# Down projections of three feed-forward layers: three of four quarters by seven block products instead of eight

## The chip, the cores and the metric

The kernel runs on one core of a Trainium2 chip. The metric is the device time of one execution in microseconds (us), smaller is better. All data are float32; the outputs are 512 tokens x 1024 features.

The core's engines are named as in the profile: PE (TensorE, matrix products into PSUM), PEld (its weight loads, which overlap PE), DVE (VectorE), ACT (ScalarE), POOL (GpSimd) and SP (SyncE, which here issues the loads from HBM). Each engine works through a queue of its own in order; where an instruction waits for another engine, everything behind it on its queue waits too.

## What is computed

Two blocks are applied to 512 tokens: the first once, the second twice (`DEPTH_2 = 2`). Each has a mixing part (attention and a linear recurrence) and then a feed-forward layer. Only the feed-forward layers are touched by the change; there are three of them, of the same shape:

```python
D_MODEL = 1024
SEQ = 512
D_FF = 4 * D_MODEL
...
        n2 = rms_norm(h, norm2_g[layer])
        h = h + jnp.square(jax.nn.relu(n2 @ w_up[layer])) @ w_down[layer]
...
    hid = jnp.square(jax.nn.relu(jnp.einsum('bsd,df->bsf', x, w_ff1)))
    ff = jnp.einsum('bsf,fd->bsd', hid, w_ff2)
    return layernorm(DEEPNORM_ALPHA * x + ff, ln2_g, ln2_b)
```

So a layer is an up projection (512 x 1024 by 1024 x 4096), a squared relu, and a down projection (512 x 4096 by 4096 x 1024), added to the residual.

## The kernel before, in words

**Matrix products.** A float32 operand x is split in two parts of a narrower kind, hi (a copy by ACT, `copy`) and lo = x - hi (a subtraction by DVE, `sub_lo`); `split2` does both. A product is then three matmuls, hi by hi, hi by lo and lo by hi, accumulated in one PSUM bank. Every matmul here takes 128 rows of contraction and writes 128 x 512.

**Weights.** `wblk` loads one block of 128 x 1024 by a DMA on SP into a tile `wr` (3 buffers), copies it into `wh` (ACT) and subtracts into `wl` (DVE). `wh` and `wl` have 6 buffers each (`NW = 6`), so weights can be split up to six blocks ahead of the block that PE works on.

**Up projection.** A block of `form_a` makes 128 of the 4096 hidden features for all 512 tokens: 8 steps of contraction x 3 matmuls = 24 matmuls from one weight block. `finish` then does relu (ACT), the square (POOL) and the split of the result into `uh` (ACT) and `ul` (DVE).

**Down projection.** `ffn` works in two halves of the hidden features: 16 up blocks, then `proj_b` twice (output columns 0 to 511 and 512 to 1023). `proj_b` holds four PSUM banks, one for each 128 tokens; each weight block covers 256 hidden features by 512 columns and feeds 2 x 3 matmuls per bank. After the last step `add_to` adds each bank to the residual tile `h` on DVE (8 additions per half).

**Who sets the order.** The order on PE is written out by hand: generators are resumed by a small planner (class `Weave`) that books costs and due times; PE then keeps that order. The order on ACT, DVE, POOL and SP is made by the scheduler of the framework, which also hands out buffers and places the semaphores. Most small tiles, activations among them, come from one pool of 56 buffers of 128 x 512 (`bt`). PSUM has 8 banks: four for projections (`mm_ps`) and four for attention and transposes (`at_ps`).

All helpers record their instructions at two places: L310 is every matmul, L262 every instruction of ACT, DVE and POOL. So rows are told apart by their tiles.

Of the kernel before, what the change touches and what calls it, by code (L numbers as in the profile page):

```python
# [11 lines left out]
F32R = mybir.dt.float32r  # L12
I32 = mybir.dt.int32
AF = mybir.ActivationFunctionType
ALU = mybir.AluOpType
# [4 lines left out]
P, T, D = 128, 512, 1024  # L20
# [133 lines left out]
class Event:  # L154


    t = None
# [110 lines left out]
def model_kernel(ctx: ExitStack, tc: tile.TileContext, I, out):  # L268
    nc = tc.nc
# [3 lines left out]
    pw = ctx.enter_context(tc.tile_pool(name="pw", bufs=NW))  # L273
# [8 lines left out]
    wv = Weave(8 - NM)  # L282
    act, dve, pool = Engine(nc.scalar, wv, 0.2, 0.83), Engine(nc.vector, wv, 0.17, 1.04), Engine(nc.gpsimd, wv, 0.25, 2.1)
    uid = [0]

    def nm(s):
        uid[0] += 1
        return f"{s}_{uid[0]}"

    def bt(s="b", dt=F32):  # L290
        return pb.tile([P, T], dt, tag="b", name=nm(s))

    def at(s="a", dt=F32):
        return pa.tile([P, 4, T], dt, tag="a", name=nm(s))
# [6 lines left out]
    def mm_ps():  # L301
        return psm.tile([P, T], F32, tag="mm", name=nm("mm"))

    def at_ps():
        t = psa.tile([P, T], F32, tag="at", name=nm("at"))
        wv.bank(t)
        return t

    def mm(out, lhsT, rhs, start, stop):
        nc.tensor.matmul(out, lhsT, rhs, start=start, stop=stop)  # L310
        n = rhs.free_size()
        if lhsT.dtype == F32:
            c = max(4 * n, 1024 if n < P else 0) * (0.5 if lhsT.free_size() <= 64 else 1.0)
        else:
            c = n if n >= 256 else 4 * n
        wv.now += c / 2400.0
# [96 lines left out]
    def proj_a(name, l, c, acts, k=8):  # L413
        ps = mm_ps()
        yield from form_a(ps, wblk(name, l, 0, k * P, c, c + P), 0, acts, range(k))
        return ps

    def proj_b(name, l, k0, k1, c, acts, done, koff=0, tail=0, wait_k=False, wait_t=False, pre=None):


        pss = [mm_ps() for _ in range(NT)]
        ks = list(range(k0 // P, k1 // P))
        steps = [ks[i : i + 2] for i in range(0, len(ks) - tail, 2)] + ([ks[len(ks) - tail :]] if tail else [])
        for st in steps:
            if pre is not None:
                pre(st[0])
            pieces = 2 if pre is not None and st[0] == 0 else 1
            ws = [wblk(name, l, k * P, (k + 2) * P, c, c + 512, pieces=pieces) for k in st[::2]]
            if pre is not None:
                pre(st[1])  # L430
            if wait_k:
                for k in st:
                    yield acts.ev[k - koff]
            for t in range(NT):
                if wait_t:
                    yield acts.ev[t]
# [174 lines left out]
    def add_to(res, n, alpha, part=None, then=None):  # L611


        def done(t, ps):
            wv.fork()
            h = res[t][n]
            if alpha == 1.0:
                dve.tensor_tensor(h, ps, h, ALU.add)
            else:
                dve.scalar_tensor_tensor(h, h, alpha, ps, ALU.mult, ALU.add)  # L620
            if part is not None:
                part(t, n)
            if then is not None:
                wv.spawn(then(t), 0)

        return done

    def out_proj(name, l, acts, res, alpha, part, then):
        yield from proj_b(name, l, 0, D, 0, acts, add_to(res, 0, alpha, part), wait_k=True)
        yield from proj_b(name, l, 0, D, 512, acts, add_to(res, 1, alpha, part, then), tail=8)  # L630

    def ffn(up, down, l, acts, res, alpha, part, then):
        for half in range(2):
            u = Acts(16, "u")

            def finish(f, ps):
                wv.fork()
                a, b = bt("ua"), bt("ub")
                act.activation(a, ps, AF.Relu)
                pool.tensor_tensor(b, a, a, ALU.mult)  # L640
                u.split(f, b)

            f0 = 0
            if half == 0:
                f0 = 4
                ws = [wblk(up, l, 0, D, P * f, P * f + P) for f in range(f0)]
                pss = [mm_ps() for _ in range(f0)]
                for j in range(2):
                    for t in range(2):
                        yield acts.ev[2 * j + t]  # L650
                    for f in range(f0):
                        yield from form_a(pss[f], ws[f], 0, acts, range(8), slice(256 * j, 256 * j + 256))
                for f in range(f0):
                    finish(f, pss[f])
            for f in range(f0, 16):
                ps = yield from proj_a(up, l, 2048 * half + P * f, acts)
                finish(f, ps)
            for n in range(2):
                last = half and n
                yield from proj_b(  # L660
                    down, l, 2048 * half, 2048 * half + 2048, 512 * n, u,
                    add_to(res, n, 1.0 if half else alpha, part if half else None, then if last else None),
                    koff=16 * half, tail=8 if last else 0, wait_k=True,
                )

    def norm_rows(g, b, l):
        return [[row_bcast(I[x], D * l + 512 * n) for n in range(2)] for x in (g, b)]
# [570 lines left out]
```

## Time and profile before

| | |
|---|---|
| median of 3 runs | 2087.22 us (2085.84 to 2088.24) |
| the profiled execution's own time | 2085.96 us |
| its span, first to last instruction | 2083.9 us |
| PE busy | 2037.8 us, 98% of the span |
| DVE busy | 939.8 us, 45% |
| ACT busy | 808.5 us, 39% |
| POOL busy | 342.7 us, 16% |
| DMA queue, share of 16 engines | 29.3% |

The three feed-forward layers are the longest stretches of the profile in which PE is never idle; between them lie the attention parts. The profile names, for every group of instructions, the busy time, the mean time of one and the idle time before it. The timeline lists single instructions with start and duration; neighbours of an engine can overlap a little, since the next one starts while the last one drains.

### The profile page before, as it was taken

The numbers are of one execution on the slowest core, as the hardware profiler recorded it, in microseconds if no ns is written. First come the engines' busy times: TensorE is split into PE (matmuls) and PEld (weight loads), VectorE is DVE, ScalarE is ACT, GpSimd is POOL, SyncE is SP. The second block draws the span as 40 slices with busy tenths as digits, with TensorE's granted clock in tenths as the row PEclk, the third lists the DMA queues.
The fourth block names the chain that finished last, engine by engine and source line by source line (L and its number), as shares of the span: only waits on it lengthen the run. The fifth ranks groups of instructions, "written<-read, shape, count | busy, mean of one in ns | idle before, by whom it ended". The sixth has DMA issues, their size and how long they took to land.

```text
span 2083.9 us, 24530 instructions
## 1 busy us (share of the span) xinstructions
PE 2037.8 (98%) x9694; PEld 1685.6 (81%) x9694; DVE 939.8 (45%) x1602; ACT 808.5 (39%) x1261; POOL 342.7 (16%) x313
## 2 busy tenths in 40 slices
PE   8999899999999999999999999999999999999998
PEld 7777778889888888877888888888877878888886
DVE  6676444544323332475555322324675554323333
ACT  6565344433422331364334322322564333322321
POOL 2000000001300210020413200311111422201302
PEclk9999999999999999999999999999999999999999
DMA  5431112242323322332232323222422233323231
GB/s 196 152 112 61 44 69 95 97 151 78 106 94 98 101 92 91 112 107 75 77 112 91 101 92 101 96 96 71 137 92 81 72 111 102 101 91 101 94 98 41
DMA packets 62371, 202.67 MB, mean 97 GB/s; under 512 B 7279, under 2 KB 7745, under 8 KB 62257
## 3 DMA queue, kind: packets, MB, share of 16 engines
q1 hardware_dynamic: 62256, 201.12, 29.3%
q8 instruction: 76, 1.25, 0.2%
q14 instruction: 39, 0.31, 0.0%
HBM read 198.94 MB, written 4.77 MB: 98 GB/s over the span
## 4 chain that ended last, share of the span: by engine, by line
PE 92%; DVE 2%; ACT 2%; POOL 2%; issue 1%; DMA 0%; POOLq 0%; ACTq 0%; DVEq 0%; SPq 0%
PE mm L310 84%; PE at L310 5%; PE at L319 2%; POOL h L262 1%; POOL mv L262 1%; ACT wh L262 0%; DVE wl L262 0%; DVE h L262 0%; ACT h L262 0%; ACT kh L262 0%; DVE og L262 0%; ACT qs L262 0%; DVE qs L262 0%; ACT sil L262 0%; DVE bs L262 0%
## 5 line engine op out<-in xcount | busy, mean ns | idle before, releaser
L262 DVE TENSOR_TENSOR wl<-wr,wh 128x1024 fp32r<-128x1024 f32 (+1 forms) x337 | 424.1, 1259 | 646.1 <-ACT wh L262 644.8
L262 ACT ACTIVATE wh<-wr 128x1024 fp32r<-128x1024 f32 (+1 forms) x340 | 358.8, 1057 | 769.9 <-PE mm L310 742.4
L310 PE MATMUL mm<-hTh,wh 128*128 128x512 f32 (+1 forms) x864 | 317.5, 367 | 0.0
L310 PE MATMUL mm<-hTl,wh 128*128 128x512 f32 (+1 forms) x864 | 316.7, 367 | 0.0
L310 PE MATMUL mm<-hTh,wl 128*128 128x512 f32 (+1 forms) x864 | 316.6, 366 | 0.0
L310 PE MATMUL mm<-wh,uh 128*128 128x512 f32 x768 | 299.1, 390 | 0.0
L310 PE MATMUL mm<-wl,uh 128*128 128x512 f32 x768 | 298.8, 389 | 0.0
L310 PE MATMUL mm<-wh,ul 128*128 128x512 f32 x768 | 298.8, 389 | 0.0
L262 POOL TENSOR_TENSOR ub<-ua 128x512 f32<-128x512 f32 x96 | 153.2, 1596 | 642.2 <-ACT ua L262 642.2
L310 PE MATMUL mm<-xTh,wh 128*128 128x512 f32 x536 | 214.1, 399 | 0.0
L310 PE MATMUL mm<-xTl,wh 128*128 128x512 f32 x536 | 209.0, 390 | 0.0
L310 PE MATMUL mm<-xTh,wl 128*128 128x512 f32 x512 | 200.0, 391 | 0.0
L310 PEld LDWEIGHTS mm<-hTl,wh 128*128 128x128 f32 x864 | 164.1, 190 | 26.1
L310 PEld LDWEIGHTS mm<-hTh,wh 128*128 128x128 f32 x864 | 164.1, 190 | 26.0
L310 PEld LDWEIGHTS mm<-hTh,wl 128*128 128x128 f32 x864 | 163.9, 190 | 26.1
L310 PEld LDWEIGHTS mm<-wl,uh 128*128 128x128 f32 x768 | 144.2, 188 | 29.9
L310 PEld LDWEIGHTS mm<-wh,ul 128*128 128x128 f32 x768 | 144.2, 188 | 29.8
L310 PEld LDWEIGHTS mm<-wh,uh 128*128 128x128 f32 x768 | 144.2, 188 | 29.7
L310 PE MATMUL mm<-wh,xTh 128*128 128x512 f32 x352 | 145.4, 413 | 12.5 <-ACT wh L262 6.5
L310 PE MATMUL mm<-wh,xTl 128*128 128x512 f32 x352 | 139.4, 396 | 0.5 <-DVE xTl L262 0.5
L310 PE MATMUL mm<-wl,xTh 128*128 128x512 f32 x352 | 139.6, 397 | 0.1
L262 DVE TENSOR_TENSOR ul<-ub,uh 128x512 fp32r<-128x512 f32 x96 | 66.4, 692 | 153.2 <-ACT uh L262 153.2
(261 smaller groups left out, 2628.7 us busy)
## 6 DMA issues: line engine op xcount, KB each, us to landing
wr<-in_wall_dram SPq DMA_DIRECT2D x338, 512.0 KB, 3.5
row<-cd SPq DMA_DIRECT2D x16, 256.0 KB, 3.9
revp<-rev SPq DMA_DIRECT2D x1, 2560.0 KB
xr<-in_xT_dram SPq DMA_DIRECT2D x8, 256.0 KB, 6.1
g<-revp SPq DMA_DIRECT2D x8, 256.0 KB, 3.9
h<-in_x_dram SPq DMA_DIRECT2D x8, 256.0 KB, 6.1
row<-in_ln_g_dram SPq DMA_DIRECT2D x8, 256.0 KB, 4.8
row<-in_ln_b_dram SPq DMA_DIRECT2D x8, 256.0 KB, 5.7
```

What stands on the lines that cost most here:

```text
L262: return f(out, *a, **k)
L310: nc.tensor.matmul(out, lhsT, rhs, start=start, stop=stop)
L319: nc.tensor.transpose(out, in_, ident)
```

## The change

In each feed-forward layer, three quarters of the hidden features (1024 of them each) no longer go through `proj_b`. For such a quarter the down projection is cut into 2 x 2 blocks in three directions: 256 tokens, 512 hidden features, 512 output columns. The plain way takes eight products of such blocks; the scheme of Strassen, here in the form with 15 additions, takes seven, of sums and differences of the blocks. The last quarter still goes through `proj_b`.

The new class `Quarter` holds one quarter:

- `load(i, j)` brings a weight block of 512 x 512 as four tiles `sw` of 128 x 512, by four DMAs.
- `put` takes an up block: relu into two tiles, `u1` (first 256 tokens) and `u2` (the others), by two ACT instructions of 128 x 256; after every second block POOL squares both tiles in place.
- `prepare(i)` makes the operands of product i: sums and differences on POOL (`combine`: 24 instructions of 128 x 512 in a quarter), then the splits, four of weights (`wh`, `wl`, 128 x 512 each) and two of activations (`xh`, `xl`).
- `product(i, add)` issues 2 x 4 x 3 = 24 matmuls into two PSUM banks. Products that share a bank go on accumulating in it (`xzzxxyv`), and after each one `add` adds the bank as it then stands to one or two residual tiles on DVE: 16 additions in a quarter.

`ffn` first makes 8 up blocks. Then for each quarter it issues, on PE, product 0, an up block of the next quarter, product 1, an up block, and so on: 7 products and 8 up blocks. The operands of product i + 1 are prepared before product i in program order. At the end comes `proj_b` for the last quarter.

```diff
+    class Quarter:
...
+        def put(self, f, ps):
+            g, c = f // 2, slice(256 * (f % 2), 256 * (f % 2) + 256)
+            if f % 2 == 0:
+                self.a1[g], self.a2[g] = bt("u1"), bt("u2")
+            wv.fork()
+            for a, h in ((self.a1[g], 0), (self.a2[g], 256)):
+                act.activation(a[:, c], ps[:, h : h + 256], AF.Relu)
+            if f % 2:
+                for a in (self.a1[g], self.a2[g]):
+                    pool.tensor_tensor(a, a, a, ALU.mult)
+                wv.mark(self.ready[g])
+        def combine(self, out, x, y, op):
+            wv.fork()
+            for o, u, v in zip(out, x, y):
+                pool.tensor_tensor(o, u, v, op)
+        def prepare(self, i):
+            a1, a2, b = self.a1, self.a2, self.b
+            lo, up = slice(0, 2), slice(2, 4)
+            sub = ALU.subtract
+            if i == 0:
+                x, w = a1[lo], b[0, 0]
+            elif i == 1:
+                self.combine(b[0, 0], b[0, 1], b[0, 0], sub)
+                self.s = [bt("us"), bt("us")]
+                self.combine(self.s, a2[lo], a2[up], ALU.add)
+                x, w = self.s, b[0, 0]
+            elif i == 2:
+                self.combine(a2[lo], a1[lo], a2[lo], sub)
+                self.combine(a1[lo], self.s, a1[lo], sub)
+                self.combine(self.s, a1[up], a1[lo], sub)
+                x, w = self.s, b[1, 1]
+            elif i == 3:
+                self.combine(b[0, 1], b[1, 1], b[0, 1], sub)
+                self.combine(b[1, 1], b[1, 1], b[0, 0], sub)
+                x, w = a1[lo], b[1, 1]
...
+            for k in range(2):
...
+                for c in range(2):
+                    d = slice(512 * c, 512 * c + 512)
+                    split2(hi[:, d], l[:, d], w[2 * k + c])
...
+            for t in x:
+                hi, l = bt("xh", F32R), bt("xl", F32R)
+                split2(hi, l, t)
...
+        def product(self, i, add):
+            xs, ws, ev = self.ops.pop(i)
+            yield ev
+            key = "xzzxxyv"[i]
...
+            for t in range(2):
+                for k in range(4):
...
+                    mm(ps[t], xh[:, c], wh[:, d], first and k == 0, False, not first)
+                    mm(ps[t], xh[:, c], wl[:, d], False, False, not first)
+                    mm(ps[t], xl[:, c], wh[:, d], False, k == 3, not first)
+                    yield 0
+                for t0, n in takes:
+                    add(t0 + t, n, ps[t], ALU.subtract if i == 5 else ALU.add)
     def ffn(up, down, l, acts, res, alpha, part, then):
-        for half in range(2):
-            u = Acts(16, "u")
...
-            for f in range(f0, 16):
-                ps = yield from proj_a(up, l, 2048 * half + P * f, acts)
+        for f in range(f0, 8):
+            ps = yield from proj_a(up, l, P * f, acts)
+            finish(f, ps)
...
+        quarters[0].prepare(0)
+        for q in range(3):
+            z = quarters[q]
+            for i in range(8):
+                if i < 6:
+                    z.prepare(i + 1)
+                elif i == 7 and q < 2:
+                    quarters[q + 1].prepare(0)
+                if i < 7:
+                    yield from z.product(i, add)
+                f = 8 * q + 8 + i
+                ps = at_ps()
+                yield from form_a(ps, wblk(up, l, 0, D, P * f, P * f + P), 0, acts, range(8))
                 finish(f, ps)
...
+        for n in range(2):
+            yield from proj_b(
+                down, l, 3072, 4096, 512 * n, u, add_to(res, n, 1.0, part, then if n else None),
+                koff=24, tail=8 if n else 0, wait_k=True,
+            )
```

In the orders below the number at the end of a name tells the tiles apart.

**DVE, second quarter of the first feed-forward layer.** Before, in an up projection, the split of a weight block (`wl<-wr`) and that of a result (`ul`) take turns:

```order
L262 TENSOR_TENSOR wl_4268<-wr_4264,wh_4265 128x1024
L262 TENSOR_TENSOR ul_3908<-ub_4166,uh_3892 128x512
L262 TENSOR_TENSOR wl_4305<-wr_4301,wh_4302 128x1024
L262 TENSOR_TENSOR ul_3909<-ub_4172,uh_3893 128x512
L262 TENSOR_TENSOR wl_4342<-wr_4338,wh_4339 128x1024
```

Of the change, from the additions after product 0 (banks 5039 and 5040) over product 1 (banks 5136 and 5137) to the split of up block 1's weights (`wl_5169`):

```order
L262 TENSOR_TENSOR h_3532<-h_3532,mm_5039 128x512
L262 TENSOR_TENSOR h_3534<-h_3534,mm_5040 128x512
L262 TENSOR_TENSOR h_3537<-h_3537,mm_5136 128x512
L262 TENSOR_TENSOR xl_5129<-us_5015,xh_5128 128x512
L262 TENSOR_TENSOR wl_5117<-sw_5102,wh_5116 128x512
L262 TENSOR_TENSOR wl_5117<-sw_5104,wh_5116 128x512
L262 TENSOR_TENSOR xl_5133<-us_5016,xh_5132 128x512
L262 TENSOR_TENSOR wl_5123<-sw_5106,wh_5122 128x512
L262 TENSOR_TENSOR wl_5123<-sw_5108,wh_5122 128x512
L262 TENSOR_TENSOR h_3539<-h_3539,mm_5137 128x512
L262 TENSOR_TENSOR wl_5169<-wr_5165,wh_5166 128x1024
```

The six splits for product 2 and the split for up block 1 now stand behind an addition that reads the first bank of product 1. The same sequence stands there in the first quarter; in the third a `ul` is in front of it.

**POOL, the same place.** Before, POOL has one square for each up block here:

```order
L262 TENSOR_TENSOR ub_4221<-ua_4220 128x512
L262 TENSOR_TENSOR ub_4258<-ua_4257 128x512
```

Of the change, from the last squares of the quarter's activations (`u_924`, `u_925`) over the combinations for products 1 and 2 to those for products 3 and 4 (`sw`):

```order
L262 TENSOR_TENSOR u_924_4952<-u_924_4952 128x512
L262 TENSOR_TENSOR u_925_4953<-u_925_4953 128x512
L262 TENSOR_TENSOR us_5016<-u_865_4615,u_925_4953 128x512
L262 TENSOR_TENSOR u_865_4615<-u_864_4614,u_865_4615 128x512
L262 TENSOR_TENSOR u_864_4614<-us_5016,u_864_4614 128x512
L262 TENSOR_TENSOR us_5015<-u_894_4790,u_832_4428 128x512
L262 TENSOR_TENSOR us_5016<-u_924_4952,u_864_4614 128x512
L262 TENSOR_TENSOR sw_4885<-sw_5102,sw_4885 128x512
L262 TENSOR_TENSOR sw_4887<-sw_5104,sw_4887 128x512
L262 TENSOR_TENSOR sw_4889<-sw_5106,sw_4889 128x512
L262 TENSOR_TENSOR sw_5102<-sw_5102,sw_4794 128x512
L262 TENSOR_TENSOR sw_4891<-sw_5108,sw_4891 128x512
```

`sw_5102` is overwritten here, and the DVE rows above read it in the fifth row: POOL has to wait for that.

**ACT, start of the first quarter.** Before, a result is copied (`uh`) as soon as it is squared. Of the change, the copies of product 0's activations (`xh_4333`, `xh_4337`) stand behind the relu of the last up block in front of it (bank 4278):

```order
L262 ACTIVATE u_794_4266<-mm_4278 128x256
L262 ACTIVATE u_795_4267<-mm_4278 128x256
L262 ACTIVATE xh_4333<-u_776_4149 128x512
L262 ACTIVATE wh_4349<-sw_4270 128x512
L262 ACTIVATE xh_4337<-u_778_4157 128x512
L262 ACTIVATE wh_4349<-sw_4272 128x512
L262 ACTIVATE wh_4355<-sw_4274 128x512
L262 ACTIVATE wh_4399<-wr_4398 128x1024
```

On PE product 0 follows that up block directly, and `wh_4399`, of the up block behind product 0, stands after a copy that waits for POOL (`sw_4274`).

## Rows read from the trace of the kernel before

**Rows 1.** The page: busy time, share and instructions of each engine; the chain.

```profile
PE 2037.8 (98%) x9694; PEld 1685.6 (81%) x9694; DVE 939.8 (45%) x1602; ACT 808.5 (39%) x1261; POOL 342.7 (16%) x313
...
PE 92%; DVE 2%; ACT 2%; POOL 2%; issue 1%; DMA 0%; POOLq 0%; ACTq 0%; DVEq 0%; SPq 0%
```

**Rows 2.** Windows: first and second feed-forward layer; stretch, length, busy (count) by engine, clock.

```profile
504.00:832.00 328.00, 328.00 (x1504) 274.00 (x1503) 105.39 (x107) 99.85 (x126) 51.07 (x32) 1.00 0.30 97
...
1115.00:1453.00 338.00, 338.00 (x1561) 282.95 (x1561) 112.39 (x119) 101.42 (x128) 56.52 (x42) 1.00 0.29 96
```

**Rows 3.** Timeline, ACT: relus of eight up blocks in a row, first and last.

```profile
545.60 0.58 ACT L262 ACTIVATE ua<-mm 128x512 f32<-128x512 f32 x1
...
583.67 0.58 ACT L262 ACTIVATE ua<-mm 128x512 f32<-128x512 f32 x1
```

**Rows 4.** Groups by shape, ACT: count, busy us, mean ns of one.

```profile
L262 ACT ACTIVATE wh<-wr 128x1024 fp32r<-128x1024 f32 x338 | 357.7, 1060 | 769.9 <-PE mm L310 742.4 <-issue 18.5 <-DMA wr<-in_wall_dram 7.4
L262 ACT ACTIVATE uh<-ub 128x512 fp32r<-128x512 f32 x96 | 60.6, 632 | 163.8 <-POOL ub L262 163.8
...
L262 ACT ACTIVATE junk<-at 128x256 f32<-128x256 f32 x16 | 6.1, 382 | 5.6 <-PE at L310 5.4
```

**Rows 5.** Groups by shape, DVE: split of an activation; addition of a PSUM bank.

```profile
L262 DVE TENSOR_TENSOR ul<-ub,uh 128x512 fp32r<-128x512 f32 x96 | 66.4, 692 | 153.2 <-ACT uh L262 153.2
L262 DVE TENSOR_TENSOR h<-mm,h 128x512 f32<-128x512 f32 x40 | 26.9, 685 | 32.1 <-PE mm L310 31.8
```

**Rows 6.** Timeline, DVE: a weight split and two splits back to back.

```profile
1466.64 1.20 DVE L262 TENSOR_TENSOR wl<-wr,wh 128x1024 fp32r<-128x1024 f32 x1
1467.76 1.28 DVE L262 TENSOR_TENSOR xTl<-at,xTh 128x512 fp32r<-128x512 f32 x2
```

**Rows 7.** Timeline, POOL: a square alone; two sums back to back.

```profile
42.45 1.04 POOL L262 TENSOR_TENSOR na<-r 128x512 f32<-128x512 f32 x1 [20.65 <-ACT r L262]
...
903.44 2.55 POOL L262 TENSOR_TENSOR cm<-row,tri 128x512 f32<-128x512 f32 x2 [10.84 <-DMA row<-cd]
```

**Rows 8.** Timeline: a POOL sum and a DVE split that meet; the split alone.

```profile
328.63 1.29 POOL L262 TENSOR_TENSOR z<-z,z 128x512 f32<-128x512 f32 x1 [29.21 <-DVE z L262]
...
328.73 2.28 DVE L262 TENSOR_TENSOR wl<-wr,wh 128x1024 fp32r<-128x1024 f32 x1 [0.18 <-ACT wh L262]
...
594.91 1.23 DVE L262 TENSOR_TENSOR wl<-wr,wh 128x1024 fp32r<-128x1024 f32 x1 [4.21 <-ACT wh L262]
```

**Rows 9.** Timeline, start of the kernel: POOL and DVE both with work queued.

```profile
16.39 5.42 POOL L262 TENSOR_TENSOR xsq<-xsq,s 128x512 f32<-128x512 f32 x3 [0.22 <-ACT s L262]
...
16.64 2.31 DVE L262 TENSOR_TENSOR wl<-wr,wh 128x1024 fp32r<-128x1024 f32 x1
18.89 3.47 DVE L262 SCALAR_TENSOR_TENSOR xTl<-xr,cols,xTh 128x512 fp32r<-128x512 f32 x2
```

**Rows 10.** Timeline: POOL at work while DVE adds a PSUM bank.

```profile
1447.59 3.17 POOL L262 TENSOR_TENSOR h<-h,row 128x512 f32<-128x512 f32 x2 [1.64 <-ACT h L262]
...
1448.21 0.69 DVE L262 TENSOR_TENSOR h<-mm,h 128x512 f32<-128x512 f32 x1
```

**Rows 11.** Windows: stretches without matmuls, and behind them; the clock is third from last.

```profile
932.56:935.50 2.94, 0.00 (x0) 0.00 (x0) 1.58 (x4) 1.96 (x4) 0.00 (x0) 1.00 0.83 325
935.78:939.19 3.41, 3.41 (x10) 2.64 (x10) 1.51 (x3) 0.71 (x2) 2.51 (x2) 0.50 0.01 2
...
1106.44:1109.86 3.42, 3.24 (x15) 3.24 (x16) 3.42 (x8) 1.54 (x2) 0.89 (x3) 0.50 0.50 158
1548.76:1551.70 2.94, 0.00 (x0) 0.00 (x0) 1.58 (x4) 1.97 (x4) 0.00 (x0) 1.00 0.89 318
1551.70:1555.10 3.40, 3.40 (x18) 2.82 (x19) 1.69 (x3) 1.34 (x3) 2.54 (x2) 1.00 0.05 18
...
1720.84:1724.26 3.42, 3.06 (x15) 3.06 (x16) 3.42 (x7) 1.54 (x2) 1.06 (x3) 0.50 0.49 158
```

More of the change, by code (lines that the diff above doesn't have):

```diff
@@ L307, in at_ps, with mm @@
         return t
-    def mm(out, lhsT, rhs, start, stop):
-        nc.tensor.matmul(out, lhsT, rhs, start=start, stop=stop)
+    def mm(out, lhsT, rhs, start, stop, more=False):
+        nc.tensor.matmul(out, lhsT, rhs, start=start, stop=stop, skip_group_check=more)
         n = rhs.free_size()
@@ L630, in out_proj @@
         yield from proj_b(name, l, 0, D, 512, acts, add_to(res, 1, alpha, part, then), tail=8)
-    def ffn(up, down, l, acts, res, alpha, part, then):
-        for half in range(2):
-            u = Acts(16, "u")
[L636 to L654, printed above, removed]
-            for f in range(f0, 16):
-                ps = yield from proj_a(up, l, 2048 * half + P * f, acts)
-                finish(f, ps)
[L658 to L664, printed above, removed]
@@ new lines, in model_kernel, with __init__, load @@
+    class Quarter:
+        def __init__(self, name, l, q):
+            self.name, self.l, self.k0 = name, l, 1024 * q
+            self.a1, self.a2 = [None] * 4, [None] * 4
+            self.b, self.banks, self.ops = {}, {}, {}
+            self.ready = [Event() for _ in range(4)]
+        def load(self, i, j):
+            self.b[i, j] = []
+            for k in range(2):
+                k0 = self.k0 + 512 * i + 256 * k
+                off, size = offs[(self.name, self.l, k0, k0 + 256, 512 * j, 512 * j + 512, "")]
+                src = I["wall"][off : off + size].rearrange("(p w) -> p w", p=P)
+                for c in range(2):
+                    t = bt("sw")
+                    load(t, src[:, 512 * c : 512 * c + 512])
+                    self.b[i, j].append(t)
+        def put(self, f, ps):
[33 more added lines that the diff above has]
+                x, w = a1[lo], b[1, 1]
+            elif i == 4:
+                x, w = a2[lo], b[0, 1]
+            elif i == 5:
+                self.combine(b[1, 1], b[1, 1], b[1, 0], sub)
+                x, w = a2[up], b[1, 1]
+            else:
+                x, w = a1[up], b[1, 0]
+            wv.fork()
+            ws = []
+            for k in range(2):
+                hi, l = pw.tile([P, 1024], F32R, tag="wh", name=nm("wh")), pw.tile([P, 1024], F32R, tag="wl", name=nm("wl"))
+                for c in range(2):
+                    d = slice(512 * c, 512 * c + 512)
+                    split2(hi[:, d], l[:, d], w[2 * k + c])
+                ws.append((hi, l))
+            xs = []
+            for t in x:
+                hi, l = bt("xh", F32R), bt("xl", F32R)
+                split2(hi, l, t)
+                xs.append((hi, l))
+            self.ops[i] = xs, ws, wv.done()
+        def product(self, i, add):
+            xs, ws, ev = self.ops.pop(i)
+            yield ev
+            key = "xzzxxyv"[i]
+            first = key not in self.banks
+            if first:
+                self.banks[key] = [mm_ps(), mm_ps()]
+            ps = self.banks[key]
+            takes = [((0, 0),), ((2, 1),), ((0, 1),), ((0, 1),), ((2, 0), (2, 1)), ((2, 0),), ((0, 0),)][i]
+            for t in range(2):
+                for k in range(4):
+                    (xh, xl), (wh, wl) = xs[k // 2], ws[k // 2]
+                    c, d = slice(256 * (k % 2) + P * t, 256 * (k % 2) + P * t + P), slice(512 * (k % 2), 512 * (k % 2) + 512)
+                    mm(ps[t], xh[:, c], wh[:, d], first and k == 0, False, not first)
[4 more added lines that the diff above has]
+                    add(t0 + t, n, ps[t], ALU.subtract if i == 5 else ALU.add)
@@ new lines, in ffn, with finish, add @@
+    def ffn(up, down, l, acts, res, alpha, part, then):
+        u, seen = Acts(8, "u"), set()
+        quarters = [Quarter(down, l, q) for q in range(3)]
+        def finish(f, ps):
+            if f < 24:
+                quarters[f // 8].put(f % 8, ps)
+                return
+            wv.fork()
+            a, b = bt("ua"), bt("ub")
+            act.activation(a, ps, AF.Relu)
+            pool.tensor_tensor(b, a, a, ALU.mult)
+            u.split(f - 24, b)
+        def add(t, n, ps, sign):
+            wv.fork()
+            h = res[t][n]
+            if alpha == 1.0 or (t, n) in seen:
+                dve.tensor_tensor(h, h, ps, sign)
+            else:
+                dve.scalar_tensor_tensor(h, h, alpha, ps, ALU.mult, sign)
+            seen.add((t, n))
+        f0 = 4
+        ws = [wblk(up, l, 0, D, P * f, P * f + P) for f in range(f0)]
+        pss = [mm_ps() for _ in range(f0)]
+        for j in range(2):
+            for t in range(2):
+                yield acts.ev[2 * j + t]
+            for f in range(f0):
+                yield from form_a(pss[f], ws[f], 0, acts, range(8), slice(256 * j, 256 * j + 256))
+        for f in range(f0):
+            finish(f, pss[f])
+        for f in range(f0, 8):
+            ps = yield from proj_a(up, l, P * f, acts)
+            finish(f, ps)
+            if f >= 6:
+                quarters[0].load(0, f - 6)
+        quarters[0].prepare(0)
[11 more added lines that the diff above has]
+                yield from form_a(ps, wblk(up, l, 0, D, P * f, P * f + P), 0, acts, range(8))
+                finish(f, ps)
+                if i in (0, 2):
+                    z.load(1, 1 if i == 0 else 0)
+                elif i in (4, 5) and q < 2:
+                    quarters[q + 1].load(0, i - 4)
+        for n in range(2):
[3 more added lines that the diff above has]
+            )
```

## The prediction

> **What bounds the kernel now.** First the page's busy times and its chain: PE is busy 98% of the span and holds 92% of the chain that ended last, while DVE has 45%, ACT 39% and POOL 16% [rows 1]. The reader should take from this that only fewer matmuls, or holes on PE, can move the time. Then the windows of the feed-forward layers: 328.00 us of 328.00 busy in the first, 338.00 of 338.00 in the second, at clock 1.00, with DVE at 105 us and POOL at 51 us there [rows 2]. So PE is saturated exactly where the change works, and any hole that appears there is new. Last the timeline, for the pace: eight relus of successive up blocks start 38.07 us apart in seven steps, so a block of 24 matmuls takes 5.44 us and one matmul 0.2266 us [rows 3].
>
> **What the change removes.** A quarter of a down projection is 192 matmuls by `proj_b` and 7 x 24 = 168 by the seven products: 24 less, in 9 quarters 216 less. 216 x 0.2266 = 48.9 us, all of it on the path as long as PE has no holes. This is all that can be gained.
>
> **What it adds, by engine and quarter.** A quarter on PE now takes 15 blocks (7 products, 8 up blocks), 15 x 5.44 = 81.6 us. On POOL the 8 squares stay and 24 sums are added. A square alone takes 1.04 us, two sums in a row 2.55 us, so 1.26 us each [rows 7]: 8 x 1.04 + 24 x 1.26 = 38.6 us. On DVE stand 28 weight splits and 14 activation splits of 128x512, 8 of 128x1024, and 16 additions. One of 128x512 takes 0.69 us alone [rows 5], 0.60 us in a row, and one of 128x1024 1.12 us in a row [rows 6]: 58 x 0.60 + 8 x 1.12 = 43.8 us. ACT copies the same tiles and has 16 short relus: 42 x 0.63 + 8 x 1.06 + 16 x 0.38 = 41.0 us at most [rows 4]. Each engine alone fits into 81.6 us, and so do the DMAs, which carry the same bytes in halves at 29% of the queue. I cost them, and the POOL sums that have no taker near, at nothing; PE's own blocks cover them. If the cover goes, the price is the stalls below.
>
> **POOL and DVE don't add up independently.** A POOL sum began at 328.63 and a DVE split with both inputs in SBUF at 328.73. The split took 2.28 us instead of the 1.23 us it takes alone [rows 8]: it waited 1.05 us, until POOL was all but done. Where both have work queued they take turns: from 18.95 to 22.36 DVE finished two splits, 1.70 us each, while POOL worked without a break [rows 9]. So a POOL instruction that gets in between costs DVE 1.1 us (1.70 less 0.60). An addition from PSUM runs freely beside POOL: 0.69 us in the middle of POOL's work [rows 10]. The Trainium skill, "SBUF — State Buffer", section "SBUF: two separate sides", says that a DVE instruction with two SBUF inputs and a GpSimd instruction exclude each other for their whole length; by that rule the sum below is 2146 us, without it the floor below, 2071 us, and rows 8 and 9 agree with it. In a quarter the two have 38.6 + 42 x 0.60 + 8 x 1.12 = 72.8 us to do one after the other, of 81.6 us. That leaves little slack for a queue that stands in a bad order.
>
> **Where PE stops.** The order on DVE has such a place. Count from the first matmul of product 0 in the second quarter: product 0, up block 0, product 1 (from 10.9), up block 1 (from 16.3, with its low weights needed at its third matmul, 16.8). On DVE the first addition of product 1 can't start before its first bank is done, at 13.6; I allow 0.2 us for the last matmul to land. Behind it stand the six splits for product 2, the second addition and only then the low weights of up block 1, `wl_5169`. That is 8 x 0.6 + 1.2 = 6.0 us, from 13.8 to 19.8: a stall of 3.0 us even with POOL silent. But POOL is not silent. It has finished `sw_4889` by then and waits for `wl_5117` before it may overwrite `sw_5102`; set free, it takes a turn before each of the next three splits (3.3 us) and a half one before the weights, since the addition hides the rest (0.5 us). 19.8 + 3.8 = 23.6, a **stall of 6.8 us**. The copies on ACT are there earlier, `wh_5169` at some 16.1: relus 0.6, six copies of 0.6 and one of 1.06 from 10.9 on [rows 4].
>
> In the third quarter a `ul` and the two POOL sums it sets free come in front: 0.6 + 2 x 1.1 more, **9.6 us**.
>
> In the first quarter nothing has been prepared ahead. Product 0 follows the last up block at once, but its activations' copies stand on ACT behind that block's relus: 0.6 for these, 0.6 for the copy, 0.7 for the split. The second pair waits on DVE for two POOL turns more, to 5.4 us where PE would want it at 1.9: 3.6 us. Up block 0's weights stand behind a copy that needs a POOL sum, then a split and a turn: ready at 11.2, wanted at 9.6, 1.6 us. For product 2 POOL has two squares and eleven sums to make since that relu, 0.6 + 2 x 1.0 + 11 x 1.26 = 16.5 us, and some eight DVE splits take turns with them, 4.8 us: 21.3. DVE can begin product 2's splits at 20.6, and with six splits, an addition, the weights and six turns (3.6 + 0.6 + 1.2 + 6.6) up block 1 has its weights at 32.6, wanted at 22.1: 10.5 us. Together **15.7 us**.
>
> After each of these PE is late and the queues have caught up; for products 3 to 6 the operands are ready at least one block early, so I cost those at nothing. The orders of the three layers are the same in kind. A layer thus stalls 15.7 + 6.8 + 9.6 = 32.1 us, three 96.3 us. With POOL silent it would be 4.4 + 3.0 + 3.6 = 11.0 us, three 33 us: the lower bound, since PE cannot pass that queue faster. As upper bound I take one more POOL turn at each of the nine places and the clock at half for twice as long: 9 x (1.1 + 1.7) = 25 us more. Of the two I take the walk with turns, since rows 8 and 9 show both engines in just this situation.
>
> **The clock.** Behind a stretch of 2.94 us without matmuls PE ran 3.41 us at clock 0.50 (1.2 GHz); behind another of the same length it stayed at 1.00 (2.4 GHz); two more stretches of 3.42 us at 0.50 stand where the norms end [rows 11]. In 3.41 us at half the clock 1.7 us are lost. Nine stalls of 7 to 10 us are longer than those; I take three in four: 9 x 1.7 x 3/4 = 11.5 us. [...]
>
> **Sum.** 2086.0 (the profiled execution's own time) - 48.9 + 96.3 + 11.5 = 2144.9 us; that execution stands 1.3 us below the median of the runs, so **2146 us**.
>
> **Rivals.**
> *POOL gives way.* If DVE, whose splits follow each other at once, keeps POOL waiting, only the floor is left: 2086.0 - 48.9 + 33 + 1.3 = 2071 us, faster. Against it stands that in rows 9 a waiting POOL got its turn each time; for it, that those rows are few and that some POOL sums may be done before the queue jams.
> *The stalls are half as long.* Some turns fall beside additions or the scheduler's queues run further ahead than I walked: halfway between floor and walk, without clock loss, 2102 us.
> *All is covered.* PE has no holes and keeps the whole gain: 2038 us. For it speaks that each engine's busy time fits. Against it, the addition in front of `wl_5169` on DVE, which no buffer takes away.
> *More places stall.* Products 3 to 5 wait too, because POOL's eight sums for product 3 and 4 start late, or weights come late on SP since `sw` tiles wait for buffers: 25 us more, 2171 us.
>
> **How the numbers follow.** A measurement of this kernel can tell about 0.2%, 4.2 us. The walk with turns, from 2115 to 2165 us, has 0.56; half-length stalls 0.13, of which 0.08 lie within 4.2 us of no change; the floor 0.19; all covered 0.03; more places 0.09. Slower: 0.56 + 0.05 + 0.09 = 0.70; faster: 0.19 + 0.03 = 0.22. The range runs from the floor, 2070 us, to 2165 us, and leaves out 0.12. The likeliest case alone has 2115 to 2165 us.
>
> **What would show it.** In the new profile: 216 matmuls less; three idle times of PE per layer at the second up block after a quarter's start, ended by DVE `wl`, of about 10, 7 and 10 us, and two short ones at the first product; splits `wl<-sw` with a mean well above 0.69 us; POOL sums near 1.8 us where they meet DVE; short stretches at clock 0.50 in layers that had none. I am wrong if PE is idle for less than 5 us per quarter, if the idle time ends on something else than DVE's weights, or if DVE's splits stay near 0.69 us although POOL works beside them.

## The result

**Slower: 2152.57 us** (median of 4 runs, 2152.07 to 2153.73) against 2087.43 us of before (4 runs in the same comparison, 2085.84 to 2088.24). The ratio is 1.0314, 95% interval 1.0296 to 1.0332. The profiled execution has a span of 2150.3 us, where that of before has 2083.9.

### The profile page after: what moved, and what is told of

The parts are those of the page before. It is cut to its first block, busy times and chain, and to the rows that moved or that the text cites. A ratio compares the mean times of both kernels' runs of the same rounds, so it can differ in the third digit from the quotient of the medians.

```text
span 2150.3 us, 25289 instructions
## 1 busy us (share of the span) xinstructions
PE 2018.1 (94%) x9478; PEld 1658.6 (77%) x9478; DVE 1253.0 (58%) x1956; ACT 907.3 (42%) x1567; POOL 654.6 (30%) x529
## 3 DMA queue, kind: packets, MB, share of 16 engines
q8 instruction: 74, 1.21, 0.2%
## 4 chain that ended last, share of the span: by engine, by line
PE 86%; DVE 6%; POOL 3%; ACT 2%; issue 2%; DMA 0%; SPq 0%; POOLq 0%; DVEq 0%; ACTq 0%
PE mm L311 60%; PE at L311 23%; DVE wl L262 3%; PE at L320 2%; POOL h L262 1%; DVE xl L262 1%; POOL us L262 1%; POOL sw L262 1%; ACT wh L262 1%; DVE h L262 0%; POOL mv L262 0%; ACT h L262 0%; POOL u L262 0%; ACT kh L262 0%; DMA xr<-in_xT_dram 0%
## 5 line engine op out<-in xcount | busy, mean ns | idle before, releaser
L262 DVE TENSOR_TENSOR wl<-sw,wh 128x512 fp32r<-128x512 f32 x252 | 253.7, 1042 | 101.3 <-ACT wh L262 99.9
L311 PE MATMUL at<-hTh,wl 128*128 128x512 f32 x576 | 233.2, 405 | 67.5 <-DVE wl L262 67.5
L262 POOL TENSOR_TENSOR sw<-sw,sw 128x512 f32<-128x512 f32 x144 | 231.0, 1633 | 171.6 <-DMA sw<-in_wall_dram 118.1
L262 ACT ACTIVATE wh<-sw 128x512 fp32r<-128x512 f32 x252 | 151.7, 628 | 215.9 <-POOL sw L262 115.5
L311 PE MATMUL at<-hTh,wh 128*128 128x512 f32 x576 | 231.5, 402 | 10.0 <-ACT wh L262 10.0
L311 PE MATMUL at<-hTl,wh 128*128 128x512 f32 x576 | 230.7, 400 | 0.0
L311 PE MATMUL mm<-wh,xl 128*128 128x512 f32 x504 | 196.8, 390 | 4.8 <-DVE xl L262 4.4
L311 PE MATMUL mm<-wh,xh 128*128 128x512 f32 x504 | 196.5, 390 | 3.8 <-ACT xh L262 3.8
L311 PE MATMUL mm<-wl,xh 128*128 128x512 f32 x504 | 196.1, 389 | 0.0
L311 PEld LDWEIGHTS at<-hTh,wh 128*128 128x128 f32 x576 | 112.9, 196 | 35.8 <-ACT wh L262 12.5
```

The lines of the kernel that those rows point to most:

```text
L262: return f(out, *a, **k)
L311: nc.tensor.matmul(out, lhsT, rhs, start=start, stop=stop, skip_group_check=more)
```

## The profile after

The page, busy time by engine and the chain, to be held against [rows 1]:

```profile
PE 2018.1 (94%) x9478; PEld 1658.6 (77%) x9478; DVE 1253.0 (58%) x1956; ACT 907.3 (42%) x1567; POOL 654.6 (30%) x529
...
PE 86%; DVE 6%; POOL 3%; ACT 2%; issue 2%; DMA 0%; SPq 0%; POOLq 0%; DVEq 0%; ACTq 0%
```

PE has 9694 - 9478 = 216 matmuls less, as counted, yet its busy share fell from 98% to 94%, and DVE and POOL now hold 9% of the chain. Windows, the first feed-forward layer's stretch of [rows 2] (length, busy time of PE, PEld, DVE, ACT and POOL with the number of instructions in brackets, clock third from last):

```profile
504.00:832.00 328.00, 299.48 (x1345) 247.02 (x1344) 201.49 (x217) 129.53 (x225) 153.35 (x104) 0.96 0.27 90
```

Where PE was busy for all of 328.00 us it now stands still for 28.5, and POOL has three times the work it had. Timeline of PE, first layer, the matmuls behind a wait of over 1 us and some of their neighbours (start, duration; in brackets the idle time before and what ended it):

```profile
542.27 0.50 PE L311 MATMUL mm<-wh,xh 128*128 128x512 f32 x1 [1.27 <-ACT xh L262]
542.61 0.40 PE L311 MATMUL mm<-wl,xh 128*128 128x512 f32 x1
...
546.26 0.50 PE L311 MATMUL mm<-wh,xl 128*128 128x512 f32 x1 [1.46 <-DVE xl L262]
...
551.89 0.50 PE L311 MATMUL at<-hTh,wl 128*128 128x512 f32 x1 [1.21 <-DVE wl L262]
...
564.84 0.79 PE L311 MATMUL at<-hTh,wh 128*128 128x512 f32 x1 [2.23 <-ACT wh L262]
...
573.00 0.80 PE L311 MATMUL at<-hTh,wl 128*128 128x512 f32 x1 [6.94 <-DVE wl L262]
...
664.10 0.79 PE L311 MATMUL at<-hTh,wl 128*128 128x512 f32 x1 [6.64 <-DVE wl L262]
664.69 0.63 PE L311 MATMUL at<-hTh,wh 128*128 128x512 f32 x1
665.11 0.63 PE L311 MATMUL at<-hTl,wh 128*128 128x512 f32 x1
...
748.10 0.50 PE L311 MATMUL at<-hTh,wh 128*128 128x512 f32 x1 [1.10 <-ACT wh L262]
...
756.35 0.79 PE L311 MATMUL at<-hTh,wl 128*128 128x512 f32 x1 [7.53 <-DVE wl L262]
```

Five holes at the start of the first quarter, one in the second, two in the third: 28.4 us in this layer. The other two layers have the same eight, within 0.5 us each; all 24 together 85.7 us. From the second start behind the hole at 664.10 on, matmuls are 0.42 us apart instead of 0.2266: half the clock. Windows of stretches at half the clock, [rows 11] being the like of before:

```profile
564.80:578.50 13.70, 6.72 (x15) 4.84 (x16) 13.70 (x12) 4.51 (x7) 10.96 (x7) 0.50 0.12 38
660.40:667.20 6.80, 3.10 (x7) 2.48 (x8) 6.80 (x7) 3.25 (x5) 4.77 (x3) 0.50 0.25 77
752.60:759.40 6.80, 3.05 (x7) 2.47 (x8) 6.80 (x7) 2.84 (x4) 4.84 (x3) 0.50 0.26 77
...
1203.10:1213.30 10.20, 3.47 (x8) 2.79 (x9) 10.20 (x8) 2.56 (x5) 9.50 (x6) 0.50 0.17 51
```

Each of the three places of each layer has one, 6.8 to 13.7 us long, in part within the hole itself.

Now the queues behind the hole of the second quarter. Timeline, DVE from the first addition of product 1 to the weights of up block 1, with the POOL and the ACT row that belong to it:

```profile
654.32 0.69 DVE L262 TENSOR_TENSOR h<-h,mm 128x512 f32<-128x512 f32 x1 [6.17 <-PE mm L311]
654.92 0.69 DVE L262 TENSOR_TENSOR xl<-us,xh 128x512 fp32r<-128x512 f32 x1
655.52 1.29 DVE L262 TENSOR_TENSOR wl<-sw,wh 128x512 fp32r<-128x512 f32 x2
656.73 1.77 DVE L262 TENSOR_TENSOR xl<-us,xh 128x512 fp32r<-128x512 f32 x1
658.42 3.41 DVE L262 TENSOR_TENSOR wl<-sw,wh 128x512 fp32r<-128x512 f32 x2
661.76 0.68 DVE L262 TENSOR_TENSOR h<-h,mm 128x512 f32<-128x512 f32 x1
662.36 1.68 DVE L262 TENSOR_TENSOR wl<-wr,wh 128x1024 fp32r<-128x1024 f32 x1
...
656.36 8.82 POOL L262 TENSOR_TENSOR sw<-sw,sw 128x512 f32<-128x512 f32 x5 [1.99 <-DVE wl L262]
...
655.27 1.05 ACT L262 ACTIVATE wh<-wr 128x1024 fp32r<-128x1024 f32 x1
```

The first three splits take 0.6 us each. The first of the two `wl` reads `sw_5102`; when it is done POOL starts, at 656.36, and from 656.73 on each split takes about 1.70 us, while the addition in the middle of POOL's work keeps its 0.68. Product 0 began at 640.5; the weights are ready at 664.04, 23.5 us later. `wh` had been there since 656.32: PE waited for DVE alone. Groups by shape (count, busy us, mean ns of one, idle time before them and its causes):

```profile
L262 DVE TENSOR_TENSOR wl<-sw,wh 128x512 fp32r<-128x512 f32 x252 | 253.7, 1042 | 101.3 <-ACT wh L262 99.9
L311 PE MATMUL at<-hTh,wl 128*128 128x512 f32 x576 | 233.2, 405 | 67.5 <-DVE wl L262 67.5
...
L262 DVE TENSOR_TENSOR h<-h,mm 128x512 f32<-128x512 f32 x128 | 85.5, 678 | 61.5 <-PE mm L311 60.8
```

A split has a mean of 1042 ns where the like of [rows 5] took 692, an addition of a PSUM bank 678 against 685. 67.5 of the 85.7 us stand before matmuls that wait for the low weights of an up block.

## The experiments

The theory (A where an expectation uses letters) is the walk of the prediction: the low weights of an up block stand on DVE behind an addition that waits for PE, behind six splits, and behind the POOL turns that come between these; the stop of PE then costs clock. All ratios are against the kernel before.

### The split of an up block's weights moved ahead

```diff
             for i in range(8):
+                f = 8 * q + 8 + i
+                wu = wblk(up, l, 0, D, P * f, P * f + P)
                 if i < 6:
                     z.prepare(i + 1)
...
-                f = 8 * q + 8 + i
                 ps = at_ps()
-                yield from form_a(ps, wblk(up, l, 0, D, P * f, P * f + P), 0, acts, range(8))
+                yield from form_a(ps, wu, 0, acts, range(8))
```

> One line is moved: the weights of an up block are requested before the operands of the next product, so that on DVE and ACT their split stands ahead of the addition after product 1 and of product 2's splits. Theory A (the stalls come from the place of that split in the queue of DVE): the long idle times of PE at the second up block of each quarter (9.2, 6.6 and 8.6 us per layer) go, and with them most of the half clock; what is left is the start of each layer's first quarter, about 4 us: 2055 to 2080 us, most likely 2065. Rival B (DVE and POOL together have too much work for a quarter, wherever it stands): PE waits as long at product 2 or 3 instead, 2130 us or more. Rival C (the weights come late from HBM or from ACT): no change, 2150 us.

Measured: 2063.25 us, ratio 0.9878 (0.9863 to 0.9892). Without a single instruction less, 89 us went, and the change became a gain. PE waits no longer at the second up block of any quarter. What stays of the first layer's holes (PE, timeline):

```profile
543.92 0.50 PE L311 MATMUL mm<-wh,xh 128*128 128x512 f32 x1 [1.78 <-ACT xh L262]
...
545.72 0.78 PE L311 MATMUL mm<-wh,xl 128*128 128x512 f32 x1 [1.07 <-DVE xl L262]
```

and three of 0.46 to 0.73 us, all in the first quarter. The turns are still there: `wl<-sw` has a mean of 1025 ns in this kernel. The turns cost PE its time because of what stood behind them.

### The sums left out

`combine` does nothing and `self.s` is `a2[lo]`: the 24 POOL sums of each quarter are left out, so the products multiply other blocks than the scheme's. Everything else stands as in the change.

```diff
             wv.fork()
-            for o, u, v in zip(out, x, y):
-                pool.tensor_tensor(o, u, v, op)
+            return
...
-                self.s = [bt("us"), bt("us")]
+                self.s = a2[lo]
```

> Left out of the computation: the 24 sums and differences of a quarter on POOL; products take the raw blocks. Squares, splits, matmuls and additions stay, and on DVE the split of the second up block's weights still stands behind the addition and product 2's splits. Theory A (the queue's order gives a floor, POOL's turns the rest): stalls at the second up block fall from 6.6 and 7.5 us to about 3 us each, 2071 to 2090 us. Rival (POOL's turns cost nothing, the order is everything): stalls of 6 us and more stay, above 2130 us. Rival (without POOL's sums nothing waits): 2038 us.

Measured: 2089.73 us (10 runs, 2084.01 to 2092.74), ratio 1.0011 (1.0002 to 1.0021); span of the profile 2082.2. DVE and PE at the second quarter's place (timeline):

```profile
640.43 0.69 DVE L262 TENSOR_TENSOR h<-h,mm 128x512 f32<-128x512 f32 x1 [7.47 <-PE mm L311]
641.03 0.69 DVE L262 TENSOR_TENSOR xl<-u,xh 128x512 fp32r<-128x512 f32 x1
641.63 1.29 DVE L262 TENSOR_TENSOR wl<-sw,wh 128x512 fp32r<-128x512 f32 x2
642.84 0.69 DVE L262 TENSOR_TENSOR xl<-u,xh 128x512 fp32r<-128x512 f32 x1
643.44 1.29 DVE L262 TENSOR_TENSOR wl<-sw,wh 128x512 fp32r<-128x512 f32 x2
644.64 0.68 DVE L262 TENSOR_TENSOR h<-h,mm 128x512 f32<-128x512 f32 x1
645.24 1.22 DVE L262 TENSOR_TENSOR wl<-wr,wh 128x1024 fp32r<-128x1024 f32 x1
...
646.52 0.50 PE L311 MATMUL at<-hTh,wl 128*128 128x512 f32 x1 [2.96 <-DVE wl L262]
```

The same nine instructions take 6.0 us instead of 9.7, and the hole is 2.96 us instead of 6.64: the floor of the walk was 3.0. So 3.7 us of that hole are POOL's turns, and 3.0 the order. All holes of the first layer here are 10.5 us (11.0 in the walk). In the profiled execution the clock fell in the layers only at the third quarters. The profiled execution is the fastest of the ten, with a granted clock of 0.989, and the runs above 2091 us have 0.985. So half the clock lasted longer in those: an estimate from the difference is 0.008 of 2090 us, 17 us at half the pace, which costs 8 us, the spread of the runs. Behind which holes, no profile shows.

### The sums on DVE

```diff
             for o, u, v in zip(out, x, y):
-                pool.tensor_tensor(o, u, v, op)
+                dve.tensor_tensor(o, u, v, op)
```

> The 24 sums and differences of a quarter are made by DVE instead of POOL; everything else as in the change, the second up block's weights still behind the addition and product 2's splits. DVE gets 24 x 0.6 = 14.4 us more per quarter (58 of 81.6 us), POOL keeps the squares. Theory A (each POOL sum holds DVE up for 1.1 us, longer than DVE would need to make it): stalls of some 3 us at the second up block of each quarter and of 3 to 5 us at the start, 2075 to 2100 us. Rival (DVE's own work binds, and more of it makes it worse): above 2160 us.

Measured: 2117.18 us, ratio 1.0138 (1.0123 to 1.0153): 35 us faster than the change, but 17 above the end of what was expected. The second up blocks wait 2.95 us as without sums (in the third quarter 1.10 and 2.47). A new hole came in (PE, timeline of the first quarter):

```profile
554.24 0.50 PE L311 MATMUL at<-hTh,wl 128*128 128x512 f32 x1 [3.98 <-DVE wl L262]
...
569.98 0.80 PE L311 MATMUL at<-hTh,wl 128*128 128x512 f32 x1 [2.95 <-DVE wl L262]
```

The sums of product 1 now stand on DVE itself, in front of the weights of up block 0: 3.98 us where the change has 1.21. And the clock is at half behind nearly all holes of the layers, also behind that of 2.95 us at 569.98. So no turns means shorter holes, but a queue in this order is full on one engine too.

### Matmuls that nobody reads, to keep PE at work

26 matmuls of 128x512 into a bank that is not read stand in front of the second up block of each quarter.

```diff
                 f = 8 * q + 8 + i
+                if i == 1:
+                    junk = at_ps()
+                    for _ in range(26):
+                        mm(junk, acts.hs[0][:, 0:P], acts.hs[0], True, True)
+                        yield 0
                 ps = at_ps()
```

> 26 matmuls of 128x512 whose result nobody reads are put on PE between product 1 and the second up block of each quarter, 5.9 us each, in the hole where PE waits for DVE. Theory (the half clock behind each stall is a cost of its own, some 18 us in the layers): the holes shrink to 0.7 to 3 us, the clock stays at 1.00 in most places, and the time falls by 10 to 18 us, to 2135 to 2143 us. Rival (clock costs nothing beyond the stall): 2152 us. Rival (PE was not idle there in truth): up by 9 x 5.9 = 53 us.

Measured: 2149.10 us, ratio 1.0288 (1.0273 to 1.0303), 3.5 us below the change: a miss. 26 matmuls are 5.9 us, and the holes of the first and third quarter were longer. Windows of this kernel: at the 4.18 us that remain in the first quarter (570.43 to 574.61), behind the 3.14 us of the third, and around the 0.86 us of the second:

```profile
573.60:580.40 6.80, 5.79 (x14) 4.53 (x15) 6.80 (x7) 3.79 (x6) 3.79 (x2) 0.50 0.25 80
...
757.90:761.30 3.40, 3.40 (x9) 2.64 (x9) 3.40 (x5) 1.58 (x2) 0.11 (x1) 0.50 0.45 158
665.00:672.00 7.00, 6.14 (x27) 4.99 (x27) 7.00 (x9) 4.05 (x8) 2.08 (x1) 1.00 0.22 77
```

The clock was kept in one of three places. This layer still has 23 matmuls in stretches at half the pace (14 + 9), and the three layers have 68 where those of the change have about 89; 21 x 0.2 us are 4 us, close to what was gained. To size the clock whole, the filling was made as long as the holes: 43, 29 and 39 matmuls in the three quarters.

```diff
-                    for _ in range(26):
+                    for _ in range((43, 29, 39)[q]):
```

> As e3_fill (2149 us), with 43, 29 and 39 unread matmuls in the first, second and third quarter instead of 26, to fill the holes at the second up block almost wholly. Theory (the half clock is a price of its own, some 18 us in all, and e3_fill kept most of it since holes of 3 to 4 us were left): no half clock behind those holes, 2132 to 2142 us. Rival (the clock is worth only the few us that e3_fill gave): 2147 to 2153 us.

Measured: 2133.81 us, ratio 1.0229 (1.0215 to 1.0243). At the second up blocks 0.39 us or less is left, and the windows behind the three places of the first layer have the full clock:

```profile
564.00:578.00 14.00, 13.62 (x61) 10.94 (x60) 14.00 (x10) 4.71 (x9) 13.17 (x8) 1.00 0.13 39
660.00:672.00 12.00, 11.82 (x52) 9.47 (x51) 11.24 (x13) 5.59 (x10) 6.84 (x5) 1.00 0.27 87
750.00:764.00 14.00, 13.79 (x61) 11.12 (x60) 12.36 (x14) 6.78 (x12) 6.13 (x4) 1.00 0.24 75
```

111 matmuls a layer, 25.2 us, stand for 24.4 us of holes, so PE is held up as long as by the holes; what differs is the clock. It is worth 2152.57 - 2133.81 = 18.8 us by the medians, and 17.7 us by the two ratios. The count agrees: the nine stretches at half the clock in the change's profile hold about 89 matmuls, each 0.2 us longer, 17.8 us.

### Product 0 prepared earlier

On top of the first experiment, the operands of the first quarter's product 0 are made before the last up block in front of it, and not behind it.

```diff
         for f in range(f0, 8):
-            ps = yield from proj_a(up, l, P * f, acts)
-            finish(f, ps)
             if f >= 6:
                 quarters[0].load(0, f - 6)
-        quarters[0].prepare(0)
+            if f == 7:
+                wu = wblk(up, l, 0, D, P * f, P * f + P)
+                quarters[0].prepare(0)
+                ps = mm_ps()
+                yield from form_a(ps, wu, 0, acts, range(8))
+            else:
+                ps = yield from proj_a(up, l, P * f, acts)
+            finish(f, ps)
```

> As e1_w_first (2063 us), and at the start of a layer's first quarter the weights and activations of product 0 are loaded and split before the last up block in front of it, so that their copies no longer stand on ACT behind that block's relus. Theory A: of the 4.6 us of idle PE that e1_w_first still has at each of the three starts, the first two holes (1.8 and 1.1 us) go, and the half clock behind them: 2046 to 2056 us. Rival (POOL's sums for product 1 are the limit there and only shift the hole): 2060 to 2064 us.

Measured: 2040.97 us (2039.40 to 2043.53), ratio 0.9782 (0.9768 to 0.9795), 5 us better than the best that was expected. One hole of 0.34 us is left in the first layer, and the clock stays full in all three.

The same edit alone, without the first experiment's:

> The change with product 0 alone prepared before the last up block; every split of an up block stands where the change has it. Theory: when up block 1's weights are ready is set by POOL's chain from the last relu (two sums and the subtraction before the wh, one turn each), and not by when product 0's blocks were made; so the two holes at the quarter's start (1.27 and 1.46 us) go, the hole before up block 1 grows by about as much in every layer, and the time falls by 0 to 5 us: 2148 to 2153 us. Rival: the holes are independent of each other; those of the quarter's start go and the others stay or shrink with the earlier start of the weights, 3 layers x 2.7 us and more with the clock: 2136 to 2145 us.

Measured: 2136.83 us, ratio 1.0231 (1.0214 to 1.0248). The rival was right, this theory of mine fell. PE, first quarter:

```profile
549.80 0.50 PE L311 MATMUL at<-hTh,wl 128*128 128x512 f32 x1 [1.60 <-DVE wl L262]
...
568.33 0.80 PE L311 MATMUL at<-hTh,wl 128*128 128x512 f32 x1 [7.35 <-DVE wl L262]
```

The two holes at the start are gone and the one before up block 1 did not grow: 9.0 us in the quarter instead of 13.1. POOL's timeline shows what the theory overlooked. Product 0's splits, once early, also set free the weight sums of product 1, and POOL has seven sums done before the squares of the last relu start at 544.04; only eight, those up to the third for product 3, stand behind them then. The chain on POOL was shorter, not only earlier.

### Do the turns matter once nobody stands behind them

The kernel with both edits, with all sums on DVE:

> As e5_early, with all sums on DVE instead of POOL. Theory A (once no weight split stands behind late work, the turns with POOL are hidden and it matters little who makes the sums): within 8 us of e5_early. Rival (POOL and DVE shutting each other out costs time everywhere): at least 10 us faster than e5_early. Rival (DVE's queue, longer by 14 us a quarter, is now the one that is late): at least 10 us slower.

Measured: 2038.18 us (2037.53 to 2038.60), ratio 0.9769 (0.9755 to 0.9782), the fastest of all. Windows, the stretch of [rows 2] once more, and DVE's group of weight splits, first of the kernel with the sums on DVE:

```profile
504.00:832.00 328.00, 328.00 (x1513) 274.07 (x1512) 216.44 (x309) 137.62 (x238) 55.57 (x32) 1.00 0.30 99
...
L262 DVE TENSOR_TENSOR wl<-sw,wh 128x512 fp32r<-128x512 f32 x252 | 166.0, 706 | 70.3 <-ACT wh L262 70.2
```

and the same group of the kernel with the sums on POOL:

```profile
L262 DVE TENSOR_TENSOR wl<-sw,wh 128x512 fp32r<-128x512 f32 x252 | 244.5, 1008 | 69.4 <-ACT wh L262 68.3
```

A split costs 302 ns less without POOL beside it, 76 us of DVE's time in all; the run is 2.8 us faster. And the profiles of the two differ ahead of the first layer already, where nothing was edited: the last hole there ends at 300.14 us in the kernel with the sums on POOL and at 297.02 in the other. With the order mended, the turns are nearly free, and this run can't tell them from nothing.

And with four sums alone on DVE, those of product 1's weights in each layer's first quarter:

```diff
-                self.combine(b[0, 0], b[0, 1], b[0, 0], sub)
+                self.combine(b[0, 0], b[0, 1], b[0, 0], sub, self.k0 == 0)
```

(`combine` uses `dve` where its last argument is true.)

> As e5_early, with only the four weight sums for product 1 of each layer's first quarter on DVE instead of POOL. There POOL has two squares and six sums to make between the last up block and product 1. Theory A (POOL's queue makes the last holes of the first quarter): 2 to 5 us faster than e5_early. Rival (those holes have another cause): within 1.5 us of it.

Measured: 2039.88 us (2038.98 to 2040.86), ratio 0.9777 (0.9764 to 0.9790). That is 1.1 us below the kernel with both edits, and the runs of the two overlap: no difference that can be told. Theory A had expected 2 to 5 us and fell: in the profile of the kernel with both edits one hole of 0.34 us was left in all three layers, so there was next to nothing to win.

## Why the prediction was right

**The gain, 48.9 us.** Right. With no hole left the run is 2038.18, and 2086.49, the median of before in that comparison, less 48.9 is 2037.6. The cover that I had costed at nothing (DVE, ACT, DMAs, the POOL sums with no taker near) held: this kernel carries the same work, with the sums on DVE, and PE is busy for 328.00 of 328.00 us; with the sums on POOL the run is 2.8 us longer.

**The second quarter, 6.8 us.** Right, step by step: DVE's addition starts 13.8 us after product 0 (13.8 walked), the weights are ready after 23.5 (23.6), the hole is 6.64. Its floor without POOL, 3.0, measured 2.96 without sums.

**The third quarter, 9.6 us.** 8.6 measured (1.10 + 7.53). The walk had not seen that part of it ends on ACT: the copy `wh` stands behind a `uh` that waits for POOL's square, 1.1 us late. The place and the rest were right.

**The first quarter, 15.7 us.** 13.1 measured. The start of product 0 took 2.7 for 3.6, up block 0 1.2 for 1.6, up block 1 9.2 for 10.5, of which 2.2 end on ACT, whose copies wait behind a POOL sum (`us`). The steps were walked a little too long: POOL's two squares and eleven sums took 20.3 us (from 541.50 to 561.78) for 20.7, and DVE from the first split for product 2 to the weights 11.7 us (from 561.28 to 572.95) for 12.0; the order of the waits was right. That the chain of sums there is anchored at the last relu was not: with product 0 made early it shrinks by itself.

**All stalls, 96.3 us.** The 24 holes are 85.7 us. A lone matmul's record is 0.39 us long where its pace is 0.2266, so each hole hides 0.16 us more: 89.6. And the matmul behind a hole is slow to let the next one start: 0.59 us at half the clock (664.10 to 664.69), where the following are 0.42 apart, and 0.34 us at the full clock (542.27 to 542.61), for 0.2266. That is 0.11 to 0.16 us a hole, 3.4 us for the 24, and makes 93.0. By the runs it is, with the clock kept 2133.81, against 2038.18 and 2040.97 with next to no holes, 93 to 96 us.

**The clock, 11.5 us: the term that was mis-sized.** It measured about 18 (18.8 by the medians). I took three in four of nine places at 1.7 us; all nine fell, and stayed low for 6.8 to 13.7 us instead of the 3.41 us of [rows 11]. The Trainium skill, "TensorE: Matmul & The Clock Gate", section "What's actually happening", says that "the default state is throttled, and activity releases the throttle". For the nine long holes the trace agrees, nine of nine. For short ones it varied, as the last section shows.

**Sum.** The walk was 6.7 us above the holes in the trace (96.3 against 89.6) and the clock 7.3 us short; that these two cancel is luck. For most of what lies between 2146 and 2152.57 the sum had no term: the 3.4 us behind the holes, and 1.6 us ahead of the first layer, where the last hole ends at 298.99 in this profile and at 297.37 in that of before. A hole of 1.94 us that both have there was followed by half the clock only in the change. Windows behind it, first before and then the change:

```profile
158.31:161.72 3.41, 3.41 (x17) 2.92 (x18) 2.86 (x11) 3.11 (x8) 0.00 (x0) 1.00 0.00 0
```

```profile
158.66:162.07 3.41, 2.95 (x9) 2.59 (x10) 2.72 (x10) 3.09 (x7) 0.00 (x0) 0.50 0.00 0
```

Some 1 us stays open. Two slips in the working move nothing: 5.4 less 1.9 is 3.5 us where the first quarter has 3.6, and halfway between 2071 and the walk without the clock, 2134.7, is 2103 us, not 2102. The rivals fell by this: POOL does take its turns (1.70 us for a split beside it, 0.60 without), which speaks against the floor of 2071 us; all three places stalled at full length, and no fourth did.

**The rule on the two engines.** The Trainium skill, "SBUF — State Buffer", section "SBUF: two separate sides", says that a DVE instruction with two SBUF inputs and a GpSimd instruction that reads SBUF exclude each other. The trace agrees: 1042 ns for a split beside POOL, 731 with the sums left out, and 678 against 683 for the addition from PSUM. That the cost then falls on PE takes the order as well: in the kernel with the weights ahead the turns remain, and 89 us are gone. The order alone, without turns, still makes 2.96 of the 6.64 us in the second quarter: the kernel without sums takes 2089.73 us, 63 less than the change but 52 more than the fastest.

## What to carry to other kernels

An engine that is busy 58% of the time can stop one that was busy 98% if its queue is in the wrong order: put what the bound engine needs next ahead of anything that waits for that engine, and ahead of preparations for later. Where work is given to a second engine, count not only its busy time but the turns that it takes from the first, and walk the queue once from the instruction that waits. Price a hole with the clock that it costs too: here about 18 us on top of the 73.8 us of holes at the second up blocks (24.4 to 24.9 us a layer).

## What I had not expected of the hardware

Half the clock lasted as long as 13.7 us where a hole came in two pieces (2.23 and 6.94 us), and in the second quarter it began while PE still stood. A short hole at one place of the program cost nothing in one kernel and much in another: before up block 1 of the first quarter PE stood still for 2.95 us both without the sums (until 561.67) and with them on DVE (until 569.98). Windows behind it, first without the sums:

```profile
561.70:568.50 6.80, 6.80 (x30) 5.64 (x31) 5.37 (x9) 1.70 (x4) 0.76 (x1) 1.00 0.46 151
```

and then with the sums on DVE:

```profile
569.00:575.80 6.80, 5.82 (x14) 4.56 (x15) 6.80 (x11) 2.74 (x4) 0.00 (x0) 0.50 0.22 77
```

30 matmuls of 0.2266 us against 14 at half the pace. What tells the two apart is open. It also makes the price of a short hole a matter of chance for a forecast, from 0 to about 2.8 us here (14 matmuls that take 0.2 us more each).
